# The order of TensorE's work around the last two attention blocks and the first GLU column tiles

## The chip, the cores and the metric

The kernel runs on one core of a Trainium2 chip. The metric is the device time of one execution in microseconds (us); of several executions the median is given. The engines are TensorE (PE, with its weight loads shown apart as PEld), VectorE (DVE), ScalarE (ACT), GpSimd (POOL) and SyncE (SP), which here issues nearly all transfers. Each engine works through its own queue in order and waits for the others by semaphores.

## The reference, cut to what matters

One layer of a decoder for a prompt of 2048 tokens and 32 sample tokens (8 sequences of 4). Attention looks back 128 tokens, so it is done in 16 blocks of 128 tokens, each against its own keys and those of the block before; beside it runs a state-space model (S5) whose output goes through a gated linear unit (GLU). Both are normalised, joined and multiplied by `w_out`; a convolutional FFN follows.

```python
h = _rmsnorm(x, p['norm_mix'])
proj = h @ p['w_in']                       # q, k, v, u
attn, k_win, v_win = attend(q, k, v, sinks)
ssm, h_re, h_im = _s5(u, ...)
ssm = jax.nn.gelu(ssm)
ssm = ssm * jax.nn.sigmoid(ssm @ p['w_glu'] + p['b_glu'])
merged = jnp.concatenate([_rmsnorm(attn, p['g_attn']), _rmsnorm(ssm, p['g_ssm'])], axis=-1)
x = x + merged @ p['w_out']
f, conv_new = _conv_ffn(_rmsnorm(x, p['norm_ffn']), ...)
x = x + f
```

Attention of a block is a softmax with a sink and a distance bias:

```python
s = jnp.einsum('bnqhgd,bnkhd->bnhgqk', qb, kband) * scale
s = s - slopes * dist
s = jnp.where(valid, s, MASK_VALUE)
p = _sink_softmax(s, sinks)
o = jnp.einsum('bnhgqk,bnkhd->bnqhgd', p, vband)
```

## The kernel before

All arrays lie with features on the 128 partitions and tokens along the free axis. A product that must keep more digits than one pass gives is split into a high and a low part of both factors and made in three passes (`mm3`, L89 to L91), so every operand has a "hi" tile, cast by ACT (L83), and a "lo" tile, subtracted by POOL or DVE (L84).

The kernel has stages. First S5's input projection; then a long stage in which q/k/v projections (`qkv`), S5 pairs and attention blocks run mixed; then the GLU, then `wo` (the product with `w_out`), then the FFN's up and down products, which take most of the time. The change lies where the mixed stage runs out into the GLU.

Each kind of work of the mixed stage is a generator, and a table of tokens, `ORDER`, says whose next step is written next: `q` a projection, `s7` a step of S5 pair 7, `a14` a step of attention block 14, `e` a gelu of one channel group, `x` a step of the sample attention, `g` one GLU column tile, `Y`, `T`, `M` and `A` the opening and closing of pools, with the norm of the first merged tile at `M`. PE executes in exactly the order in which the steps are written. The order of the other engines is set by a scheduler from the program's dependencies, so it follows the table, but not word for word.

An attention block (`attention_block`) has five steps. Steps 1 and 2 are the two key/value heads: 12 score matmuls each (`sc_b`) into two PSUM banks of the pool `psa`, which has only these two; DVE adds the bias and takes the maximum (L545); then `softmax` negates the maximum (`ngm`, L510, DVE), takes four exponentials with their sums on ACT (L513, `den`) and one of the sink (L516), adds and inverts on DVE (L517, L518) and multiplies on POOL (L520). `ngm`, `den` and `es` have two buffers each. Steps 3 and 4 transpose the probabilities of a head (`tp_b`, L556, 8 transposes) and copy them out (`pT_b`, L561). Step 5 multiplies by the values (`o`, L567) and ACT copies the result (`osb`, L570, one buffer) for a transfer to `mscr`.

The gelu of a channel group (`gelus`, L947 and L950) reads `y`, writes four buffers `gt`, and sends them to `gscr`. The GLU (`glu_tiles`) runs over 8 token tiles of 260 with 4 column tiles each, 32 steps `g`. For a token tile it loads `gel` (L958, three buffers) from `gscr`, which needs the gelus of all four channel groups, and casts it to `ghi` and `glo`; a column tile is 12 matmuls into one of two PSUM banks, then ACT's tanh (L1029), two DVE operations (L1030, L1031) and a transfer to `mscr` (L1032) from one of three buffers `sg`. The weights of `wo` are loaded in 8 parts (L932); the first three are split by ACT and DVE, the last five by DVE alone (L83, L84). `merged_sums` loads a merged tile (`mt`, L989) and squares it, `merged_norm` makes the factor from a matmul `st_m`, on ACT and DVE.

```python
for tok in ORDER.split():
    ...
    else:
        next(steps[tok])
```

Of the kernel before, what the change touches and what calls it, by code (L numbers as in the profile page):

```python
# [51 lines left out]
a4 s8 a4 a6 s7 a5 s9 q a6 s9 s8 s10 s9 q a5 a5 a6 q a7 s10 s9 s10 q s11 a6 a7 a6 s11 q s11 a7 q s10 s12 a7 a7  # L52
s12 a8 s11 q s13 s12 q q a8 q s13 s12 s13 a8 a9 s14 q a8 s14 a9 q s13 a8 s14 s15 s15 a10 a9 q a9 a9 s15 q s14
a10 q s15 a11 a10 a11 a10 q a10 q q Y a11 a11 a12 a11 q a13 q a12 q a12 q q q e e a12 a13 a12 a14 a13 e e T a13
a13 x g a14 g g x a14 a15 g a14 g g x g a15 x g a14 g g g g a15 g g g g g g g M a15 g g a15 g g g g g g g g g g
g A
"""
WOAT = 9
GELQ = lambda nc: (nc.sync, nc.scalar)[GELQI]
# [1615 lines left out]
```

## Time and profile before

| | us |
|---|---|
| median of 3 runs | 2193.05 (2192.98 to 2195.53) |
| the profiled execution | 2194.39 |
| its span, first to last instruction | 2192.2 |
| PE busy in the span | 2054.4 (94%) |
| DVE, ACT, POOL busy | 1307.6, 1055.8, 1208.9 |

The profile gives a start and a length to every instruction of one execution. A row of a timeline merges like instructions that follow each other; a bracket at its end says how long the engine was idle before and whose work ended that. Names are those of the program without numbers. Matmuls overlap, so the time of one step is best read from the start of one group to the start of the next. A table of stretches gives each engine's busy time, the granted clock of PE (1.00 is 2.4 GHz, 0.50 is 1.2 GHz) and the share of the transfer engines. The chain that ended last is followed back from the last instruction.

### The profile page before, as it was taken

To read this page: it belongs to the slowest core of one execution; us is meant where nothing else is said; L and a number is where in the kernel's file an instruction comes from. 1 tells how busy PE (TensorE), PEld (TensorE's weight loads), DVE (VectorE), ACT (ScalarE), POOL (GpSimd) and SP (SyncE) were. 2 spreads that over 40 slices of the span, in tenths; PEclk is the share of its full clock that TensorE was granted. 3 is DMA by queue.
4 is the path that set the end of the run, shared out by engine and by line. 5 is a ranking of instruction groups with operands and counts; after the bars stand their busy time and mean duration, and the time that the engine had idled before them with its cause. 6 is when DMAs were issued, how large, how long until landed. Compare 5 with 4: busy or idle time off the path is not lost.

```text
span 2192.2 us, 41498 instructions
## 1 busy us (share of the span) xinstructions
PE 2054.4 (94%) x14685; PEld 1923.5 (88%) x14685; DVE 1307.6 (60%) x3298; ACT 1055.8 (48%) x2467; POOL 1208.9 (55%) x1196
## 2 busy tenths in 40 slices
PE   8969999968999979999999998999999999999997
PEld 8967878857998979999999786779999999888997
DVE  8859998458565576766766265227766766601231
ACT  6525465665454456666666332225655655612011
POOL 4857776334356776666665553446666666823121
PEclk9989999989999989999999999999999999999999
DMA  8865434686488733333334795834333333584643
GB/s 232 240 169 158 116 106 138 125 230 189 146 248 258 262 109 109 113 95 109 114 95 128 263 284 170 303 117 157 110 93 108 111 93 108 177 205 125 199 132 95
DMA packets 294352, 347.59 MB, mean 159 GB/s; under 512 B 42344, under 2 KB 250864, under 8 KB 294128
## 3 DMA queue, kind: packets, MB, share of 16 engines
q1 hardware_dynamic: 294144, 344.94, 52.3%
q8 instruction: 116, 1.90, 0.4%
q14 instruction: 92, 0.75, 0.1%
HBM read 232.70 MB, written 107.80 MB: 155 GB/s over the span
## 4 chain that ended last, share of the span: by engine, by line
PE 75%; DVE 8%; DMA 6%; issue 4%; ACT 3%; POOL 3%; SPq 2%; DVEq 0%; ACTq 0%; POOLq 0%
PE ux L1362 21%; PE u L1362 16%; PE dn L90 6%; PE dn L89 6%; PE dn L91 6%; PE wo L90 2%; PE wo L91 2%; PE wo L89 2%; PE qkv L89 2%; PE qkv L91 1%; PE qkv L90 1%; DVE xo L1444 1%; SPq L802 1%; PE u L91 1%; DMA mt<-mscr 1%
## 5 line engine op out<-in xcount | busy, mean ns | idle before, releaser
L84 POOL TENSOR_TENSOR wdl<-wdr,wdh 128x1024 fp32r<-128x1024 f32 x65 | 159.3, 2455 | 287.3 <-ACT wdh L83 272.0
L89 PE MATMUL dn<-ah,wdh 128*128 128x512 f32 (+3 forms) x552 | 205.6, 372 | 8.9 <-DMA ah<-actscr 3.6
L91 PE MATMUL dn<-ah,wdl 128*128 128x512 f32 (+3 forms) x552 | 205.1, 371 | 3.3 <-POOL wdl L84 3.3
L90 PE MATMUL dn<-al,wdh 128*128 128x512 f32 (+3 forms) x552 | 204.9, 371 | 0.5 <-DMA al<-actscr 0.5
L1327 ACT ACTIVATE cc<-u,cw 128x260 f32<-128x260 f32 (+1 forms) x252 | 141.5, 563 | 93.8 <-DVE u L1405 64.1
L1519 DVE TENSOR_TENSOR xo<-xo,dn 128x512 f32<-128x512 f32 (+3 forms) x40 | 21.9, 584 | 265.4 <-PE dn L91 265.1
L83 ACT CAST wdh<-wdr 128x1024 fp32r<-128x1024 f32 x65 | 68.0, 1050 | 230.4 <-PE dn L90 188.4
L84 POOL TENSOR_TENSOR wls<-s,whs 128x1024 fp32r<-128x1024 f32 x42 | 100.9, 2402 | 133.2 <-ACT whs L83 133.2
L1328 DVE SCALAR_TENSOR_TENSOR cc<-u,cw,cc 128x260 f32<-128x260 f32 (+1 forms) x252 | 121.0, 481 | 64.2 <-ACT cc L1327 62.7
L89 PE MATMUL wo<-mh,wo 128*128 128x260 f32 x512 | 149.0, 291 | 2.5 <-ACT mh L83 2.5
L90 PE MATMUL wo<-ml,wo 128*128 128x260 f32 x512 | 146.7, 287 | 1.5 <-POOL ml L84 1.3
L91 PE MATMUL wo<-mh,wo 128*128 128x260 f32 x512 | 146.4, 286 | 0.0
L1405 DVE TENSOR_TENSOR u<-u,cb 128x262 f32<-128x262 f32 x84 | 36.5, 435 | 158.5 <-PE u L1362 158.5
L89 PEld LDWEIGHTS dn<-ah,wdh 128*128 128x128 f32 x552 | 105.1, 190 | 28.7 <-issue 4.0
L91 PEld LDWEIGHTS dn<-ah,wdl 128*128 128x128 f32 x552 | 105.1, 190 | 20.8 <-POOL wdl L84 4.2
L89 PE MATMUL qkv<-hh_p,wqh 128*128 128x256 f32 (+1 forms) x384 | 113.5, 296 | 10.6 <-DVE vs L905 7.4
L84 POOL TENSOR_TENSOR wlt<-s,wht 128x512 fp32r<-128x512 f32 x42 | 54.1, 1288 | 122.6 <-ACT wht L83 64.0
L90 PEld LDWEIGHTS dn<-al,wdh 128*128 128x128 f32 x552 | 105.1, 190 | 17.6 <-DMA al<-actscr 1.0
L1329 DVE SCALAR_TENSOR_TENSOR cc<-u,cw,cc 128x260 f32<-128x260 f32 (+1 forms) x252 | 119.6, 475 | 0.8
L84 POOL TENSOR_TENSOR wlg<-wur,whg 128x1024 fp32r<-128x1024 f32 x42 | 101.1, 2407 | 27.8 <-ACT whg L83 27.8
L520 POOL TENSOR_SCALAR s_b<-s_b,den_b 128x256 f32<-128x256 f32 x128 | 75.4, 605 | 63.2 <-DVE den_b L518 38.4
L90 PE MATMUL qkv<-hl_p,wqh 128*128 128x256 f32 (+1 forms) x384 | 109.9, 286 | 0.0
(574 smaller groups left out, 8370.9 us busy)
## 6 DMA issues: line engine op xcount, KB each, us to landing
actscr<-cc SPq DMA_DIRECT2D x168, 260.0 KB, 4.9
wur<-in_w_up SPq DMA_DIRECT2D x84, 512.0 KB, 4.1
wdr<-in_w_down SPq DMA_DIRECT2D x77, 512.0 KB, 4.9
x<-in_xT SPq DMA_DIRECT2D x56, 256.0 KB, 4.2
hs<-h2scr SPq DMA_DIRECT2D x44, 262.0 KB, 4.6
ah<-actscr SPq DMA_DIRECT2D x42, 256.0 KB, 3.9
al<-actscr SPq DMA_DIRECT2D x42, 256.0 KB, 4.2
mt<-mscr SPq DMA_DIRECT2D x16, 520.0 KB, 5.5
```

The source lines that it names most:

```text
L83: i = nc.scalar.copy(hi, src) if hi_eng is nc.scalar else hi_eng.tensor_copy(hi, src)
L84: return i.ins, lo_eng.tensor_tensor(lo, src, hi.bitcast(F32), ALU.subtract).ins
L89: nc.tensor.matmul(ps, w[0], x[0], start=first, stop=False)
L90: nc.tensor.matmul(ps, w[0], x[1], start=False, stop=False)
L91: nc.tensor.matmul(ps, w[1], x[0], start=False, stop=last)
L520: nc.gpsimd.tensor_scalar(s[:, h], s[:, h], den[:, h : h + 1], 1.0, ALU.mult, ALU.mult)
L802: nc.sync.dma_start(uscr[8 * m + g].rearrange("(s h) c -> h s c", h=16), uperm[m][16 * g : 16 * g + 16])
L1327: nc.scalar.activation(cp, pp[:, 2:], AF.Identity, bias=w[3], scale=w[2])
L1328: nc.vector.scalar_tensor_tensor(cp, pp[:, 1 : npr + 1], w[1], cp, ALU.mult, ALU.add)
L1329: nc.vector.scalar_tensor_tensor(cp, pp[:, 0:npr], w[0], cp, ALU.mult, ALU.add)
L1362: nc.tensor.matmul(pt[:, :W], x[p][:, k], y[q][:, k], start=start and k + i == 0, stop=k == 3 and i == 2, skip_group_check=True)
L1405: v.tensor_tensor(c21[s], c21[s], cb[s][:, 0], ALU.add)
```

## The change

Two lines of `ORDER` are replaced; no other line of the program differs..

```diff
 ...
-a13 x g a14 g g x a14 a15 g a14 g g x g a15 x g a14 g g g g a15 g g g g g g g M a15 g g a15 g g g g g g g g g g
-g A
+a13 a15 a14 a15 a14 a14 g x g a15 a14 g g x g a15 g x g g a15 x g g g g g g g g g g M g g g g g g g g g g g g
+g g A
```

Block 14 has made its first step before these lines and has four left, block 15 all five. Before, the first GLU tile followed block 13's output, and the steps of the two blocks stood one by one between GLU tiles, the last one behind the 21st. Now the three remaining score steps and both transposes of block 14 stand ahead of the first GLU tile, and the last step of either block behind the eighth. The norm of the first merged tile (`M`) stands behind the 18th GLU tile and not behind the 19th; the sample attention's steps move by up to one GLU tile.

On PE, at the place where the mixed stage ends (`o_13` is the output of block 13, `sc_b14_1` the scores of block 14's second head, `tp_` transposes, `glu_0_2` token tile 0, column tile 2, `ssc` the samples' scores; of each group of matmuls its first row), before:

```order
L567 MATMUL o_13_6966<-pT_b13_0_0_6871,vtok_6_0_6141 64x512
L89 MATMUL glu_0_0_7003<-ghi_0_0_6987,wgh0_6926 128x260
L89 MATMUL sc_b14_1_0_7023<-kp10_2167,q0_7_6452 128x256
L89 MATMUL glu_0_1_7057<-ghi_0_0_6987,wgh1_6934 128x260
L89 MATMUL glu_0_2_7075<-ghi_0_0_6987,wgh2_6940 128x260
L604 MATMUL ssc_0_7099<-kc_6978,qs_2188 32x288 x4
L556 MATMUL tp_b14_0_0_7123<-ident_201,s_b14_0_6830 128x128 x4
L89 MATMUL sc_b15_0_0_7139<-kp10_2167,q0_7_6452 128x256
L89 MATMUL glu_0_3_7173<-ghi_0_0_6987,wgh3_6946 128x260
L556 MATMUL tp_b14_1_0_7191<-ident_201,s_b14_1_7021 128x128 x4
L89 MATMUL glu_1_0_7223<-ghi_1_0_7207,wgh0_6926 128x260
```

and now, at the same place:

```order
L567 MATMUL o_13_6966<-pT_b13_0_0_6871,vtok_6_0_6141 64x512
L89 MATMUL sc_b15_0_0_6976<-kp10_2167,q0_7_6452 128x256
L89 MATMUL sc_b14_1_0_7012<-kp10_2167,q0_7_6452 128x256
L89 MATMUL sc_b15_1_0_7048<-kp10_2167,q0_7_6452 128x256
L556 MATMUL tp_b14_0_0_7082<-ident_201,s_b14_0_6830 128x128 x4
L556 MATMUL tp_b14_1_0_7096<-ident_201,s_b14_1_7010 128x128 x4
L89 MATMUL glu_0_0_7126<-ghi_0_0_7110,wgh0_6926 128x260
L89 MATMUL glu_0_1_7157<-ghi_0_0_7110,wgh1_6934 128x260
L556 MATMUL tp_b15_0_0_7175<-ident_201,s_b15_0_6974 128x128 x4
L567 MATMUL o_14_7189<-pT_b14_0_0_7087,vtok_6_1_6145 64x512
L89 MATMUL glu_0_2_7197<-ghi_0_0_7110,wgh2_6940 128x260
L89 MATMUL glu_0_3_7215<-ghi_0_0_7110,wgh3_6946 128x260
```

Three score groups and block 14's transposes have gone from between the GLU tiles to ahead of them.

On ACT, at the same place (the exponentials of blocks 14 and 15, the table load and the gelus of channel group 2), the difference:

```order
 L513 ACTIVATE s_b14_0_6830,den_b14_0_6852<-s_b14_0_6830,ngm_b14_0_6850 128x256 x4
 L516 ACTIVATE es_b14_0_6857<-es_b14_0_6857 128x4
+L513 ACTIVATE s_b15_0_6974,den_b15_0_6996<-s_b15_0_6974,ngm_b15_0_6994 128x256 x4
+L516 ACTIVATE es_b15_0_7001<-es_b15_0_7001 128x4
+L513 ACTIVATE s_b14_1_7010,den_b14_1_7032<-s_b14_1_7010,ngm_b14_1_7030 128x256 x4
+L516 ACTIVATE es_b14_1_7037<-es_b14_1_7037 128x4
+L513 ACTIVATE s_b15_1_7046,den_b15_1_7068<-s_b15_1_7046,ngm_b15_1_7066 128x256 x4
+L516 ACTIVATE es_b15_1_7073<-es_b15_1_7073 128x4
 L947 ACT_TABLE_LOAD
 L947 ACTIVATE gt_2_0_6880<-y_2_6741 128x512
```

Three groups of exponentials now stand ahead of the table load of the gelus, which they followed before.

On DVE, near the end of the GLU (`sg_6_3` is the gate of token tile 6, column 3; `wo06` and `wo16` are the high and low part of the seventh part of `w_out`), before:

```order
L1030 TENSOR_SCALAR sg_6_3_7978<-sg_6_3_7978 128x260
L1030 TENSOR_SCALAR sg_7_0_8012<-sg_7_0_8012 128x260
L1031 TENSOR_TENSOR sg_6_3_7978<-sg_6_3_7978,gel_6_7795 128x260
L1031 TENSOR_TENSOR sg_7_0_8012<-sg_7_0_8012,gel_7_7893 128x260
L83 CAST wo06_8105<-wor6_8107 128x1024
L1030 TENSOR_SCALAR sg_7_1_8030<-sg_7_1_8030 128x260
L84 TENSOR_TENSOR wo16_8106<-wor6_8107,wo06_8105 128x1024
L1031 TENSOR_TENSOR sg_7_1_8030<-sg_7_1_8030,gel_7_7893 128x260
L1117 MEMSET hs_0_0_8884 128x2x2
L83 CAST wo07_8111<-wor7_8113 128x1024
L84 TENSOR_TENSOR wo17_8112<-wor7_8113,wo07_8111 128x1024
L1030 TENSOR_SCALAR sg_7_2_8048<-sg_7_2_8048 128x260
```

and now:

```order
L1030 TENSOR_SCALAR sg_6_1_7942<-sg_6_1_7942 128x260
L1031 TENSOR_TENSOR sg_6_1_7942<-sg_6_1_7942,gel_6_7803 128x260
L83 CAST wo06_8105<-wor6_8107 128x1024
L84 TENSOR_TENSOR wo16_8106<-wor6_8107,wo06_8105 128x1024
L1030 TENSOR_SCALAR sg_6_2_7960<-sg_6_2_7960 128x260
L1030 TENSOR_SCALAR sg_6_3_7978<-sg_6_3_7978 128x260
L1031 TENSOR_TENSOR sg_6_2_7960<-sg_6_2_7960,gel_6_7803 128x260
L1031 TENSOR_TENSOR sg_6_3_7978<-sg_6_3_7978,gel_6_7803 128x260
L83 CAST wo07_8111<-wor7_8113 128x1024
L1117 MEMSET hs_0_0_8884 128x2x2
L84 TENSOR_TENSOR wo17_8112<-wor7_8113,wo07_8111 128x1024
L1030 TENSOR_SCALAR sg_7_0_8012<-sg_7_0_8012 128x260
```

The last two splits of `w_out` have moved from behind the gates of `sg_7_0` and `sg_7_1` to ahead of those of `sg_6_2` and `sg_7_0`.

On SP, at the first column of `wo` (`x2scr` takes the result of that column, `xm` is the residual stream loaded for later columns, `mt_1` the second merged tile), before:

```order
L1193 DMA x2scr_63<-xm_0_0_8138 128x260
L1187 DMA xm_1_4_8715<-in_xT 128x260
L1187 DMA xm_1_5_8744<-in_xT 128x260
L1187 DMA xm_1_6_8799<-in_xT 128x260
L989 DMA mt_1_0_8167<-mscr_62 128x4x260
L989 DMA mt_1_4_8169<-mscr_62 128x4x260
```

and now:

```order
L1032 DMA mscr_62<-sg_7_2_8048 128x260
L1032 DMA mscr_62<-sg_7_3_8066 128x260
L1193 DMA x2scr_63<-xm_0_0_8138 128x260
L989 DMA mt_1_0_8167<-mscr_62 128x4x260
L989 DMA mt_1_4_8169<-mscr_62 128x4x260
```

The three loads of `xm` stand with eight others in one row further up, ahead of the write of `sg_4_2`.

## Rows read from the trace of the kernel before

**Rows 1.** The page: the chain that ended last, shares of the span by engine.

```profile
PE 75%; DVE 8%; DMA 6%; issue 4%; ACT 3%; POOL 3%; SPq 2%; DVEq 0%; ACTq 0%; POOLq 0%
```

**Rows 2.** Timeline of PE: start, length, instruction, count, idle before.

```profile
448.74 3.68 PE L567 MATMUL o<-pT_b,vtok 128*64 128x512 f32 x8
465.57 0.59 PE L89 MATMUL glu<-ghi,wgh 128*128 128x260 f32 x1 [13.14 <-ACT ghi L83]
...
468.69 0.41 PE L89 MATMUL sc_b<-kp,q 128*128 128x256 f32 x1
...
470.62 0.28 PE L89 MATMUL glu<-ghi,wgh 128*128 128x260 f32 x1
...
474.34 1.09 PE L556 MATMUL tp_b<-ident,s_b 128*128 128x128 f32 x8
476.27 0.39 PE L89 MATMUL sc_b<-kp,q 128*128 128x256 f32 x1 [0.83 <-DVE sm L606]
...
477.81 0.28 PE L89 MATMUL glu<-ghi,wgh 128*128 128x260 f32 x1
...
479.25 1.94 PE L556 MATMUL tp_b<-ident,s_b 128*128 128x128 f32 x8
480.94 0.37 PE L89 MATMUL glu<-ghi,wgh 128*128 128x260 f32 x1
```

**Rows 3.** Timeline of ACT, from block 14's exponentials to the second table load.

```profile
444.81 0.51 ACT L513 ACTIVATE s_b<-s_b,ngm_b 128x256 f32<-128x256 f32 x1 [0.32 <-DVE ngm_b L510]
...
446.80 0.19 ACT L516 ACTIVATE es_b<-es_b 128x4 f32<-128x4 f32 x1
447.00 1.28 ACT L947 ACT_TABLE_LOAD   x1
...
455.24 0.58 ACT L570 COPY osb<-o 128x512 f32<-128x512 f32 x1 [2.60 <-DMA mscr<-osb]
456.00 1.12 ACT L947 ACTIVATE gt<-y 128x512 f32<-128x512 f32 x1 [0.18 <-DMA gscr<-gt]
...
457.17 3.11 ACT L947 ACTIVATE gt<-y 128x512 f32<-128x512 f32 x3
...
465.11 1.33 ACT L83 CAST ghi<-gel 128x260 fp32r<-128x260 f32 x4 [4.32 <-DMA gel<-gscr]
...
473.43 1.28 ACT L513 ACT_TABLE_LOAD   x1
```

**Rows 4.** Stretches: length, busy time of each engine (instructions), PE clock, DMA share, GB/s.

```profile
465.57:493.88 28.31, 27.22 (x216) 23.43 (x216) 22.92 (x75) 19.49 (x55) 12.58 (x20) 0.93 0.74 222
493.88:514.17 20.29, 18.14 (x142) 17.11 (x141) 14.37 (x29) 11.68 (x35) 13.28 (x17) 1.00 0.79 231
514.17:547.40 33.23, 26.47 (x179) 22.93 (x177) 30.76 (x53) 16.32 (x37) 13.37 (x16) 0.95 0.55 165
...
466.00:467.00 1.00, 1.00 (x5) 0.97 (x5) 0.00 (x0) 0.44 (x2) 1.00 (x2) 0.50 0.72 196
```

**Rows 5.** Timelines of DVE (first two) and POOL: a reduction, the hole, a normalisation.

```profile
442.26 0.48 DVE L545 CUSTOM_DVE_ANT_0 s_b<-sc_b,bias,sink 128x256 f32<-128x256 f32 x1 [1.59 <-PE sc_b L91]
...
460.82 0.69 DVE L84 TENSOR_TENSOR wgl<-wgraw,wgh 128x512 fp32r<-128x512 f32 x1 [11.20 <-ACT wgh L83]
...
449.81 1.84 POOL L520 TENSOR_SCALAR s_b<-s_b,den_b 128x256 f32<-128x256 f32 x4 [2.38 <-DVE den_b L518]
```

**Rows 6.** DVE's groups from 465.5 to 550: busy us and mean ns, then idle before.

```profile
L561 DVE COPY pT_b<-tp_b 128x512 f32<-128x512 f32 x8 | 5.4, 682 | 0.0
L545 DVE CUSTOM_DVE_ANT_0 s_b<-sc_b,bias,sink 128x256 f32<-128x256 f32 x12 | 5.3, 473 | 0.0
```

**Rows 7.** Timelines of SP (first row) and PE, in the first tile of `wo`.

```profile
551.29 1.61 SPq L1187 DMA_DIRECT2D xm<-in_xT  x3
...
561.11 0.71 PE L115 MATMUL st_m<-ss_m,ones 128*128 128x260 f32 x2 [2.04 <-POOL ss_m L134]
563.55 1.24 PE L115 MATMUL st_m<-ss_m,ones 128*128 128x260 f32 x2 [1.74 <-POOL ss_m L134]
```

## The prediction

> **What bounds the kernel now.** I read the page first: TensorE (PE) holds 75% of the chain that ended last [rows 1], so a change pays only where PE stands still, and only if nothing else is late then. The one large hole in reach of the change is in the timeline of PE: the output matmuls of attention block 13 start at 448.74 and take 3.68 us, and the next thing in PE's order, the first GLU column tile, starts at 465.57 after 13.14 us of idleness put down to ACT's cast of `ghi` [rows 2]. The timeline of ACT tells why [rows 3]: exponentials of block 14 until 446.99, a table load at 447.00, the gelus of channel groups 2 and 3 (with the copy of block 13's output between them, which waits 2.60 us for its buffer to be written back), the last gelu ending at 460.28, and then 4.32 us of waiting until the gelu output has gone to memory and come back as `gel`. So PE waits for a chain of ACT and DMA that begins where the exponentials end. What follows, from 465.57 to the first `wo` matmul at 547.40, has three parts in the table of stretches [rows 4]. Up to 493.88 PE is busy 27.22 of 28.31 us and sets the pace. From there to 514.17 it is busy 18.14 of 20.29. In the last 33.23 us DVE is busy 30.76 and PE only 26.47: DVE sets the pace there, through the GLU gate, the norm of the first merged tile and the splitting of the `wo` weights.
>
> **The change, part by part.** Nothing is added or removed. Three score groups, the transposes of block 14 and, a little, those of block 15 move ahead on PE; the scheduler then places the other engines' work by that order.
>
> *The hole.* PE can start block 15's first scores at 452.42. The hole covers PE's part: twelve score matmuls take 477.81 − 476.27 = 1.54 us at the full clock [rows 2], and DVE is idle there for 11.20 us [rows 5]. It does not cover ACT's part. The order of ACT puts the three groups of exponentials ahead of the gelu table load, and the whole chain to the first GLU tile hangs on that load. First scores of six matmuls are there about 1.1 us after 452.42; four reductions of 0.48 us, a little overlapped [rows 5], end at 455.3; the first reduction of the next group stands ahead of the negated maximum, so the exponentials begin at about 456.2. One group costs ACT 446.99 − 444.81 = 2.18 us [rows 3]; three without a gap would end at 462.8. The third must wait longer, because `den` has two buffers and the first group's is free only after POOL has normalised it: about 459.5 plus 1.84 us [rows 5], so 461.4 + 2.18 = 463.6. The table load thus moves from 447.00 to about 463.6, 16.6 us later. Of this the chain gets back 2.60 + 0.18 us of waiting [rows 3], since block 13's output and the buffers of the gelus are long ready by then: 13.8 us net, and the first GLU tile starts at 479.4. The bounds are 12.2 (no reduction in between, no wait for POOL) and 15.2 (scores at half clock, which cost 470.62 − 468.69 = 1.93 us a group partly at that level [rows 2], and some wait for the gelu buffers remaining). PE still waits some 16 us in place of 13, so its first GLU tile still starts, as before, at a granted clock of 0.50, the lower of the two levels, 1.2 GHz [rows 4].
>
> *The GLU stretch, first part (28.31 us).* It loses a score group of 1.93, the transposes, the wait of 0.83 and the score group from 474.34 to 477.81, 3.47, transposes of 480.94 − 479.25 = 1.69 [rows 2], and a last score group like the one of 1.54: together 8.6 us. It takes in block 15's transposes (two times about 1.0, as the row of 1.09) and output (1.84, half of the 3.68 at half clock), 3.9 us that stood in the later parts. Two waits are new, where the moved scores had been cover: about 1.0 us for the low part of the second weight column, and about 2 us for the sample softmax, whose two ACT operations and table load (1.28 [rows 3]) now follow a cast that needs the third `gel`, itself queued on SP behind block 14's output. So 28.3 − 8.6 + 3.9 + 2.9 = 26.5 us.
>
> *Second part (20.29 us).* It loses one pair of transposes (about 0.8 after overlap) and one GLU tile (1.45), as the norm is now called one column earlier; it gains some wait, since the loads of the first merged tile follow closer on the sample output: bounds 0 and 3, I take 0.5, near zero, because these loads had only small waits before. 18.5 us.
>
> *Third part (33.23 us).* One GLU tile more, transposes and output of block 15 fewer: on DVE that cancels. But in the new order all five weight splits stand ahead of the gate of the last four GLU tiles, where two splits stood behind two of them. One split is about 1.9 us of DVE, so 0 to 3.8 us; I take 1.5, since in the old order, too, one split stood ahead of the last tiles: 34.7 us.
>
> The three parts make 79.7 against 81.83: 2.1 us come back. Behind the first `wo` column SP no longer has three loads of `xm`, 1.61 us, ahead of the loads of the second merged tile, and PE's two waits of 2.04 and 1.74 us for its sums [rows 7] shrink by as much: 1.6 us. The order of all that follows is the same. **Sum: 13.8 − 2.1 − 1.6 = 10.1 us slower.** The span of 2192.2 becomes 2202.3, and the profiled execution's 2194.39 us becomes 2204.5. That execution stands 1.3 us over the median of 2193.05, so I predict 2203.
>
> A rule for such an order: ACT's two table loads at 447.00 and 473.43 cost 1.28 us each [rows 3], and the second serves the exponentials of block 14 and of the samples. The Trainium skill (ScalarE: Activation LUTs, Table sets: the hidden batching unit) asks to batch activation calls by table set, which this change does for block 14 and 15. By that rule a load of 1.28 us would go, and the sum would be 8.8; by the order it stays, as the sample softmax still comes behind the gelus, and I leave the sum at 10.1.
>
> **The rivals.** *Given back.* The stretch returns all 8.6 us of PE work with no new wait, and the delay is at its lower bound: 12.2 − 8.6 − 1.6 = +2.0, to +3.6 with the central delay: 2195 to 2197. For it speaks that DVE loses 5.3 us of reductions and half of the 5.4 us of copies [rows 6]; against it, that most of this work stood in the first part, where PE and not DVE sets the pace.
>
> *Faster.* PE runs the stretch without waits: it is busy 71.8 us in it (the sum of [rows 4]), about 7.8 of that leave, and 81.8 − 64.0 = 17.8 us would come back, with the 1.6 us 19.4: 13.8 − 19.4 = −5.6, some 2187. It decides from the point where the stretch gives back more than 13.8 us. Against it speaks the 30.76 us of DVE in the last part, which the change leaves as they are.
>
> *More is lost.* The bare GLU tiles wait for each other: there are three `sg` buffers, and SP now has eleven loads of `xm`, some 0.54 us each by [rows 7], in one row ahead of the write that frees one of them: up to 5.9 us, so that the stretch gives nothing back or loses some: +14 to +18, 2207 to 2211. The Trainium skill (Perfetto Trace Analysis, Optimization Strategy) says that regimes with different most-contended engines may be run interleaved to advantage; the old order does so with attention and GLU, and by that rule this rival would be the likely one. Rows speak for it only in part: the two regimes are bound by PE and then by DVE [rows 4], but attention lay mostly within PE's.
>
> That the change does not do what it says is excluded: the order of PE shows the three score groups where they are claimed to be.
>
> **How the numbers follow.** The delay seems certain, since the place of the exponentials ahead of the table load is fixed in ACT's order; how much the stretch returns is not. Forecast, +5 to +14 (2198 to 2207): 0.63. Given back: 0.17. More is lost: 0.15. Faster: 0.05. The range of 2195 to 2209 takes in the forecast, most of the second and half of the third. A measurement of this kernel can tell about 0.2%, 4.4 us, from no change: slower by more 0.78, within 0.17, faster 0.05.
>
> **What would show it.** In the profile of the changed kernel: the gelu table load at about 463 in place of 447; the first GLU tile at about 479 after a wait of PE for `ghi` of some 16 us, with nothing of the transposes behind it; the stretch from there to the first `wo` matmul about 80 us; the wait for the sums of the second merged tile under 2.5 us in all; everything behind shifted by the same 10 us. I would be wrong in the first step if the gelus began before 458, in the second if the stretch took under 75 us or over 85.

## The result

The changed kernel takes 2205.8 us (median of six runs, 2202.62 to 2210.42), the kernel before 2194.06 beside it: ratio 1.0052, 95% interval 1.0036 to 1.0067, so 11.7 us slower. Run again in the experiments it was 1.0056 (1.0039 to 1.0074). The forecast was 2203, from 2195 to 2209. The executions of one kernel lie 4 to 21 us apart within a set. The two traces of the changed kernel come from executions of 2208.8 and 2202.8 us, on either side of its median, and differ by 3.4 us in the stretch that matters here; differences of that size between single traces say nothing. Where it matters I use both and several of the old order.

**The hole.** The timeline of PE after, from the second transposes of block 13 to the first GLU tile (columns as in [rows 2]):

```profile
449.12 2.35 PE L556 MATMUL tp_b<-ident,s_b 128*128 128x128 f32 x8 [2.31 <-POOL s_b L520]
...
454.77 0.39 PE L89 MATMUL sc_b<-kp,q 128*128 128x256 f32 x1
...
456.75 0.39 PE L89 MATMUL sc_b<-kp,q 128*128 128x256 f32 x1 [0.28 <-DVE m_b L545]
...
458.78 0.39 PE L89 MATMUL sc_b<-kp,q 128*128 128x256 f32 x1 [0.25 <-DVE m_b L545]
...
464.47 2.69 PE L556 MATMUL tp_b<-ident,s_b 128*128 128x128 f32 x8 [2.95 <-POOL s_b L520]
481.65 0.58 PE L89 MATMUL glu<-ghi,wgh 128*128 128x260 f32 x1 [14.49 <-ACT ghi L83]
```

and of ACT in the same place, where [rows 3] had the load at 447.00:

```profile
458.43 0.51 ACT L513 ACTIVATE s_b<-s_b,ngm_b 128x256 f32<-128x256 f32 x1 [8.45 <-DVE ngm_b L510]
...
463.58 0.51 ACT L513 ACTIVATE s_b<-s_b,ngm_b 128x256 f32<-128x256 f32 x1 [0.81 <-DVE den_b L517]
...
465.77 1.28 ACT L947 ACT_TABLE_LOAD   x1
...
471.27 0.57 ACT L570 COPY osb<-o 128x512 f32<-128x512 f32 x1
471.73 1.12 ACT L947 ACTIVATE gt<-y 128x512 f32<-128x512 f32 x1
...
481.19 2.17 ACT L83 CAST ghi<-gel 128x260 fp32r<-128x260 f32 x6 [4.67 <-DMA gel<-gscr]
```

The three score groups run in the hole, as the change says. ACT then stands idle 8.45 us, does their exponentials and only then loads the gelu table. This execution was already 3.0 us late before the change's place (the transposes of block 13 start at 449.12, before at 446.13), so I measure from there: the first GLU tile comes after 32.53 us in place of 19.44, the hole is 13.1 us longer.

**The rest.** The stretches after, to be held against [rows 4]; the last row reaches from the first `wo` matmul to the first addition of the second token tile:

```profile
481.65:510.76 29.11, 27.34 (x187) 22.04 (x188) 18.95 (x41) 14.96 (x34) 9.31 (x12) 0.83 0.76 225
510.76:532.09 21.33, 17.71 (x122) 17.20 (x121) 10.58 (x23) 11.05 (x27) 9.02 (x12) 0.84 0.79 232
532.09:567.94 35.85, 26.35 (x174) 24.98 (x173) 31.98 (x56) 16.77 (x38) 15.21 (x16) 0.86 0.55 167
567.94:597.07 29.13, 27.24 (x224) 26.77 (x223) 12.52 (x34) 14.33 (x37) 12.58 (x18) 1.00 0.40 125
```

The same in the second trace of the changed kernel:

```profile
478.31:505.44 27.13, 24.43 (x187) 19.09 (x187) 19.66 (x42) 15.04 (x34) 9.31 (x12) 0.94 0.83 250
505.44:523.89 18.45, 15.50 (x122) 14.73 (x121) 11.34 (x21) 10.90 (x27) 9.53 (x12) 1.00 0.84 244
523.89:561.42 37.53, 26.38 (x174) 25.01 (x173) 31.65 (x56) 16.75 (x38) 15.36 (x16) 0.86 0.54 167
561.42:590.31 28.89, 27.26 (x224) 26.79 (x223) 12.50 (x33) 14.86 (x39) 13.01 (x18) 1.00 0.40 126
```

and the last stretch before, which [rows 4] do not have:

```profile
547.40:581.22 33.82, 30.04 (x225) 29.23 (x224) 14.76 (x36) 15.12 (x39) 13.58 (x19) 0.90 0.46 140
```

From the first GLU tile to the second token tile of `wo` that is 115.42 and 112.00 us after, 115.65 before. PE lost work there (8.3 us of busy time in the second trace, 3.2 in the first, where more of it ran at the half clock), but its idle time, length less busy time, rose from 13.8 to 16.8 us, and to 18.4 in the second trace. What PE waits for, before and then after (us in total, times, longest):

```profile
PE glu L89 <- ACT sg L1029: 6.4, 8, 2.2
```

```profile
PE glu L89 <- ACT sg L1029: 12.6, 5, 4.0
```

Eight small waits for the tanh have become five, three of them long, and a stretch behind the first of these shows the half clock (columns as in [rows 4]). In the second trace the same three tiles waited 2.71, 4.80 and 4.85 us.

```profile
523.69 0.58 PE L89 MATMUL glu<-ghi,wgh 128*128 128x260 f32 x1 [3.58 <-ACT sg L1029]
...
540.08 0.58 PE L89 MATMUL glu<-ghi,wgh 128*128 128x260 f32 x1 [4.05 <-ACT sg L1029]
...
558.31 0.58 PE L89 MATMUL glu<-ghi,wgh 128*128 128x260 f32 x1 [3.88 <-ACT sg L1029]
```

```profile
524.00:529.00 5.00, 5.00 (x24) 5.00 (x24) 2.74 (x6) 1.65 (x5) 2.22 (x4) 0.50 0.54 164
530.00:532.00 2.00, 2.00 (x19) 2.00 (x19) 1.60 (x4) 0.56 (x2) 0.52 (x1) 1.00 0.46 141
```

### The profile page after: what moved, and what is told of

It reads as the page before. It is cut to its first block, busy times and chain, and to the rows that moved or that the text cites. A ratio compares the mean times of both kernels' runs of the same rounds, so it can differ in the third digit from the quotient of the medians.

```text
span 2207.0 us, 41497 instructions
## 1 busy us (share of the span) xinstructions
PE 2055.4 (93%) x14685; PEld 1925.7 (87%) x14685; DVE 1308.4 (59%) x3298; ACT 1057.1 (48%) x2467; POOL 1211.0 (55%) x1196
## 4 chain that ended last, share of the span: by engine, by line
PE 60%; DVE 3%; POOL 3%; DMA 2%; issue 2%; ACT 2%; SPq 0%; DVEq 0%; POOLq 0%; ACTq 0%
PE ux L1362 20%; PE u L1362 16%; PE dn L89 7%; PE dn L90 7%; PE dn L91 7%; PE wo L90 1%; PE wo L91 1%; PE wo L89 1%; DVE xo L1444 1%; POOL ml L84 1%; DMA wdr<-in_w_down 1%; DVE xm L1159 0%; POOL wd L84 0%; DMA mt<-mscr 0%; DVE ss_fo L134 0%
## 5 line engine op out<-in xcount | busy, mean ns | idle before, releaser
L91 PE MATMUL qkv<-hh_p,wql 128*128 128x256 f32 (+1 forms) x384 | 110.2, 287 | 0.0
```

The lines of the kernel that those rows point to most:

```text
L91: nc.tensor.matmul(ps, w[1], x[0], start=False, stop=last)
```

## The experiments

My theory after the result had two parts: the exponentials ahead of the gelu table load make the first GLU tile late, and the stretch gives nothing back because bare GLU tiles run into three waits for the tanh. The rivals: a late start itself makes the stretch long; PE sets its pace; VectorE (DVE) does.

One table for all runs. Each ratio is to the kernel before on the same chip. **Hole**: from PE's second transposes of block 13 to its first GLU matmul. **Train**: from there to the end of the last gate (DVE, L1031). **To wo 2**: from the first GLU matmul to DVE's first addition for the second token tile of `wo` (L1192).

| kernel | ratio (95%) | hole | train | to wo 2 |
|---|---|---|---|---|
| before | | 19.44 | 84.57 | 115.65 |
| changed | 1.0052 (1.0036–1.0067) | 32.53 | 87.88 | 115.42 |
| e12 changed again | 1.0056 (1.0039–1.0074) | 32.13 | 84.76 | 112.00 |
| e2 before, gelus delayed | 1.0067 (1.0042–1.0092) | 36.25 | 85.35 | 117.30 |
| e1 changed, gelus first | 1.0037 (1.0024–1.0050) | 22.94 | 92.70 | 121.51 |
| e5 before, one group moved | 1.0054 (1.0042–1.0066) | 25.88 | 90.66 | 120.92 |
| e6 changed, cover at the norm | 1.0049 (1.0032–1.0065) | 33.56 | 85.81 | 113.27 |
| e3 changed, 5 sg | 1.0045 (1.0029–1.0061) | 32.13 | 82.01 | 111.31 |
| e7 changed, squares later | 1.0057 (1.0044–1.0071) | 33.50 | 85.92 | 115.27 |
| e9 e3, e6 and later squares | 1.0061 (1.0043–1.0078) | 32.07 | 86.54 | 117.72 |
| e10 changed, 9.2 us of PE work added | 1.0068 (1.0049–1.0088) | 32.29 | 86.01 | 115.12 |
| e4 before, 5 sg | 0.9999 (0.9987–1.0011) | 17.55 | 86.29 | 115.86 |
| e11 before, PE's idle places filled | 1.0016 (1.0000–1.0032) | 18.34 | 84.70 | 114.15 |
| e13 before, wo splits off DVE | 1.0007 (0.9994–1.0019) | 18.80 | 85.89 | 117.93 |

Hole plus the last column, held against before's 135.09, agrees with the ratios within 3 us (changed: +12.9 beside 11.4), but for e2 and e12, which are 3 to 4 off, and e11 with 6. From the second token tile of `wo` to its last addition all traces take 175 to 178 us: the change is decided by then.

**e2: a delay alone.** The order before; 28 copies on ACT ahead of the gelus of group 2.

```diff
+NDUM = 28
 ...
+                for _ in range(NDUM if (m, i) == (2, 0) else 0):
+                    nc.scalar.copy(gt[:, 0:512].rearrange("p (t c) -> p t c", t=8), y[:, :, 0:64])
```

> The order of the kernel before; 28 added copies of 128x512 on ScalarE ahead of the gelus of channel group 2 delay the chain to the first GLU tile, with nothing moved. At some 0.59 us each they are 16.5 us, less the 2.8 us of waits that the chain had: the first GLU tile 13 to 14 us later. My theory (a delay of the chain goes through to the end in full, and the stretch does not depend on when it begins): stretch 81 to 83 us, time 2206 to 2208, ratio 1.0055 to 1.0065. Rival (a late start makes the stretch itself longer, as in the changed kernel): stretch 86, time 2211 to 2213. Rival (work that does not hang on the chain goes on meanwhile, and part of the delay is given back): 2198 to 2202.

ACT (first two rows) and PE of e2 (its lines behind the edit stand up to three higher):

```profile
453.96 15.55 ACT L949 COPY gt<-y 128x512 f32<-128x512 f32 x24
...
473.10 1.12 ACT L950 ACTIVATE gt<-y 128x512 f32<-128x512 f32 x1 [1.82 <-DMA gscr<-gt]
```

```profile
482.78 0.58 PE L90 MATMUL glu<-ghi,wgh 128*128 128x260 f32 x1 [30.64 <-ACT ghi L84]
```

The copies were dearer than I had reckoned, 0.65 us each and not 0.59, and of the 2.8 us of waits 1.82 remained: the first GLU tile came 16.8 us later. The medians differ by 2211.84 − 2194.96 = 16.9 us. The ratio gives 14.7, because one of the six executions took 2195.82 us, about as long as the kernel before, and the other five 2211.4 to 2215.7; why that one was fast is not known. The time is in the range of the first rival, but not for its reason: the delay was 3 us larger than planned, and the stretch to the first `wo` tile took 83.18 us, near the theory's 81 to 83 and not 86. The train took 85.35 us beside 84.57. So a delay of the gelu chain goes through about in full, and a late start does not make the stretch long by more than two traces differ.

**e1: the gelus first.** The changed order of PE; the three moved softmaxes are held behind the last gelu on ACT.

```diff
+GFIRST = ("b14_1", "b15_0", "b15_1")
 ...
-        softmax(c, pool, s, m, 4, c.sink[:, 4 * kv : 4 * kv + 4], nm)
+        with c.tc.issue_after(c.last_gelu) if nm in GFIRST else nullcontext():
+            softmax(c, pool, s, m, 4, c.sink[:, 4 * kv : 4 * kv + 4], nm)
 ...
```

(The rest of the edit keeps the last gelu as `c.last_gelu`.)

> The order of TensorE is that of the changed kernel; only ScalarE is changed: the exponentials of blocks 15_0, 14_1 and 15_1 are held behind the last gelu. My theory has two parts: the first GLU tile is late because these exponentials stand ahead of the gelu table load, and the stretch from the first GLU tile to the first wo tile is long (86.3 us in the changed kernel, 81.83 before) because the bare GLU tiles run into ScalarE. By it the table load is back at 447 to 450, the first GLU tile starts at 469 to 471 (three groups of 2.18 us and a table load of 1.28 now stand between the last gelu and the casts of gel), the stretch stays at 85 to 87, and the time is some 11 us under the changed kernel's: 2194 to 2197, ratio 1.000 to 1.0015. Rival: the stretch was long because it began late; then it goes back to about 80 and the time is 2187 to 2190. Second rival: something else makes the first GLU tile late, and it stays at about 481, 2205.

ACT (first two rows) and PE of e1 (its lines stand one or two higher):

```profile
449.16 1.28 ACT L949 ACT_TABLE_LOAD   x1
...
470.77 1.94 ACT L84 CAST ghi<-gel 128x260 fp32r<-128x260 f32 x6
```

```profile
468.56 2.69 PE L558 MATMUL tp_b<-ident,s_b 128*128 128x128 f32 x8 [7.72 <-POOL s_b L521]
471.21 0.58 PE L90 MATMUL glu<-ghi,wgh 128*128 128x260 f32 x1
473.99 0.58 PE L91 MATMUL glu<-glo,wgh 128*128 128x260 f32 x1 [2.20 <-DVE glo L85]
...
476.65 0.58 PE L91 MATMUL glu<-glo,wgh 128*128 128x260 f32 x1 [0.99 <-POOL glo L85]
```

The table load is back at 449 and the first GLU tile at 471, as forecast: 9.6 of the 13.1 us came back, so the place of the exponentials made it late. But the gain did not last: 2203.56 us, not 2194 to 2197. The same exponentials now stand ahead of the casts of `gel`, the first tile starts and stops for its low parts, and the train is 92.7 us (90.76 to the first `wo` tile, where 85 to 87 was expected). The hole was one of PE and DVE; ACT's idle times in it, 2.60 us ahead of the last gelus and 4.32 behind them [rows 3], are each too short for three groups of 2.18 us.

**e5: one group.** The order before with only block 15's first scores moved ahead.

```diff
-a13 x g a14 g g x a14 a15 g a14 ...
+a13 a15 x g a14 g g x a14 g a14 ...
```

> The order of the kernel before with one step moved: only the first score group of block 15 goes ahead of the first GLU tile, the other two stay between the tiles. Theory (each group whose exponentials stand ahead of the gelu table load delays the first GLU tile): one group, so the table load at about 458 to 459 in place of 447, the first GLU tile 8 to 10 us later, at 474 to 476; the stretch to the first wo tile loses one score group and stays at 79 to 81; time +6 to +9 over the kernel before: 2201 to 2204, ratio 1.003 to 1.004. Rival (the delay of the changed kernel came from all three groups together, through the wait for POOL and den's two buffers, and one group fits beside the gelus): first GLU tile within 2 us of before, 2193 to 2196.

```profile
473.36 0.58 PE L89 MATMUL glu<-ghi,wgh 128*128 128x260 f32 x1 [19.04 <-ACT ghi L83]
...
487.67 0.33 PE L556 MATMUL tp_b<-ident,s_b 128*128 128x128 f32 x1 [2.33 <-POOL s_b L520]
```

The table load came at 457.84, as forecast, and the hole grew by 6.4 us, less than the 8 to 10 expected and half of what all three groups cost. The time did not follow: 2207.7 us where 2201 to 2204 was expected, ratio 1.0054, as slow as all three groups. The train took 90.66 us; PE waited 2.8 us for block 14's probabilities and 5.0 us for POOL's `glo` in it. So the loss is not one share per group. Why a single group lengthens the train by 6 us is not shown.

**e6, e3, e7, e9: the three waits.** e6 puts block 15's second transposes and output back behind the norm, e3 gives `sg` five buffers, e7 puts the first merged tile's squares later on ACT, e9 does all three (the squares less late, offset −60).

```diff
-... x g a15 g x g g a15 x g g g g g g g g g g M g g g g g g g g g g g g
+... x g g x g g x g g g g g g g g g g M a15 g g a15 g g g g g g g g g g
```

```diff
-                    sg = st.gl2.tile([P, n], F32, tag="sg", name=f"sg_{it}_{m}", bufs=3)
+                    sg = st.gl2.tile([P, n], F32, tag="sg", name=f"sg_{it}_{m}", bufs=5)
```

```diff
+SQP = -400
 ...
-                        st.sums = merged_sums(0, st.ms)
+                        with tc.high_priority(offset=SQP):
+                            st.sums = merged_sums(0, st.ms)
```

> The changed kernel with one piece put back: the second transposes and the output of block 15 stand again behind the norm of the first merged tile (one directly behind it, the other two GLU tiles later), as in the kernel before. My theory: these 3 us of TensorE work covered the time in which ScalarE does the norm's logarithms and exponentials with its two table loads; without them TensorE waited 4.05 us and ran one or two GLU tiles at half clock after it. By it this wait falls under 1 us, the first GLU tile stays at 480 to 482, and the time is 4 to 5 us under the changed kernel's: 2200 to 2202, ratio 1.003. Rival: VectorE sets the pace of the last part (31.98 of 35.85 us busy), and what TensorE does not wait there it waits later: 2204 to 2207, ratio 1.005.

> The changed kernel with five sg buffers in place of three. ScalarE's tanh waited 5.72, 2.48 and about 1 us for the write that frees an sg buffer, and TensorE 3.88 us behind the first of these, with two tiles at half clock after it. Theory A: the ring of three holds TensorE up; the wait of 3.88 goes, and the time is 4 to 6 us under the changed kernel's: 2200 to 2202. Theory B: the tanh is early then, but the gates behind it wait for VectorE, which splits weights: the wait of TensorE goes all the same, since only the tanh frees its bank, but the first merged tile's norm or the wo weights are late instead, and the time moves by less than 2 us: 2204 to 2207.

> The order of TensorE of the changed kernel; the eight squares of the first merged tile stand some four GLU tiles later in the order of ScalarE, where in the changed kernel they stood, waiting for their load, ahead of the tanhs that free TensorE's banks. Theory: the wait of 3.58 us at 523.69 goes, and with it the two GLU tiles at half clock after it; the middle part (to the norm's sums) falls from 21.3 to 16 to 18 us and the first wo tile is 4 to 6 us earlier. In the time a part of this may be given back at the sums of the second merged tile, as with five sg buffers: 2201 to 2204, ratio 1.003 to 1.004. Rival: the sums are then late for the norm, and TensorE waits there as long: 2205 to 2207.

> The changed kernel with all three waits of the stretch treated at once: block 15's second transposes and output back behind the norm, five sg buffers, and the squares of the first merged tile two GLU tiles later on ScalarE. The first GLU tile is as late as in the changed kernel (479 to 482). Theory: the three waits of 3.6 to 4.1 us and the half-clock tiles behind them made the stretch long; it falls from 86.3 to 74 to 77 us, less than the 81.83 of before by the score groups that left it. The sums of the second merged tile then take back some 4 us: time 2198 to 2201, ratio 1.002 to 1.003. Rival: the stretch has a floor of DVE work at about 80 us, and the time is 2203 to 2206.

Each did what it should at its wait: e6 cut the norm's from 4.05 to 1.78 us, e3 the last from 3.88 to 1.74, e7 the first from 3.58 to 0.16. None changed the time by more than the intervals: 2205.3 and 2204.6 us for e6 and e3, as the rival and theory B had said, 2208.4 for e7, above even its rival, and 2211.4 for e9, with all of them (1.0061), above both its ranges. The waits turned up elsewhere: e6 waits 4.30 us at the squares, e3 4.46 and e7 4.84 us at the norm, e9 5.3 us for POOL's `glo`. Only e3's train was clearly shorter in its trace (82.01), and its `wo` part gave much of that back (34.33 us from the first `wo` matmul, 29.13 in the changed kernel). The theory's second part falls: shortening these waits, one by one or together, does not shorten the time.

**e10: PE work added.** The changed kernel with six groups of twelve matmuls that nobody reads, 9.2 us, in pairs ahead of the three tiles that waited.

```diff
-... M g g g g g g g g g g g g
-g g A
+... M
+g g d d g g g g g g g d d g g g g g A
```

(and one pair four tiles ahead of `M`; `d` writes an unread `sc` bank.)

> The changed kernel with six score groups (twelve matmuls of 128x256 each, 1.54 us at the full clock, 9.2 us in all) added on TensorE whose result nobody reads: two ahead of each of the three GLU tiles that waited 3.58, 4.05 and 3.88 us for the tanh. Theory (the stretch is paced by the casts, gates and splits around the GLU tiles; TensorE's work there lies in gaps, so the 6.7 us of score groups and transposes that the change took out brought nothing back): the added 9.2 us cost nothing, and if the half-clock tiles behind the waits count, up to 5 us come back: 2199 to 2206, ratio 1.002 to 1.0055. Rival (TensorE sets the pace): +6 to +9 on the changed kernel, 2212 to 2215, ratio 1.008 to 1.0095.

The last stretch of e10 ahead of `wo` (columns as in [rows 4]), then SP and PE at the start of `wo` (first matmul 561.92):

```profile
532.00:561.92 29.92, 26.13 (x205) 24.86 (x205) 25.08 (x45) 14.39 (x35) 12.91 (x16) 1.00 0.42 130
```

```profile
565.58 0.33 SPq L1032 DMA_DIRECT2D mscr<-sg  x1
...
570.11 1.10 SPq L989 DMA_DIRECT2D mt<-mscr  x2
```

```profile
577.46 1.24 PE L115 MATMUL st_m<-ss_m,ones 128*128 128x260 f32 x2 [3.84 <-POOL ss_m L134]
579.77 1.24 PE L115 MATMUL st_m<-ss_m,ones 128*128 128x260 f32 x2 [1.08 <-POOL ss_m L134]
```

The three waits shrank to 1.24 us at most and the granted clock was 1.00 in the whole last third. PE reached its first `wo` matmul 80.4 us after the first GLU tile, in place of 86.3 and 83.1, with 9.2 us more to do. But the last gate came after 86.0 us all the same, so the last `sg` write and the loads of the second merged tile stood later against PE, and PE waited for their sums. To the second token tile it took 115.12 us. The time, 2210.2 us and 1.0068, lies between the two ranges: above the theory's 2199 to 2206, below the rival's 2212 to 2215. It is 2.6 us by the ratio over the second run of the changed kernel, with intervals that overlap widely; the rival's 6 us more would be 1.0083, which the interval just takes in. So the time alone does not decide; the trace does: 9.2 us more work left the train and the way to the second token tile as long as in the two traces of the changed kernel, within 3.2 us. **PE's work is not what paces the second and third part of the stretch**, so taking it out there could give little back. The first part got no added work.

**e4, e11, e13: other limits, on the kernel before.** e4: five `sg`. e11: ten unread groups, eight in the hole, two at the sums of the second merged tile. e13: five of the ten `wo` split steps of DVE to ACT, two to POOL.

```diff
-a13 x g a14 g g x ...
+a13 d d d d d d d d x g a14 g g x ...
 ...
```

```diff
-WOE = ((1, 1), (1, 1), (1, 1), (1, 1), (1, 1))
+WOE = ((0, 1), (0, 2), (0, 1), (0, 2), (0, 1))
```

> The kernel before with five sg buffers in place of three. Theory: its waits for the tanh in the last part (1.62 and 2.17 us, with a half-clock tile after the second) go, the stretch falls from 81.83 to 77 to 79 us; of this the wait for the sums of the second merged tile takes back half or more, since their loads stand behind the last sg writes in SP's queue: 2191 to 2195, ratio 0.998 to 1.000. Rival: nothing is taken back, 2188 to 2190, ratio 0.997.

> The kernel before with ten unread groups of twelve matmuls added on TensorE only where it stands still: eight in the hole ahead of the first GLU tile (12.3 of its 13.1 us) and one ahead of each of the two sums of the second merged tile (waits of 2.04 and 1.74 us). Theory (the half clock behind these waits is what TensorE pays for its idleness): the first GLU tile takes 1.7 us in place of 3.3, the first wo tile behind the sums 1.6 and 1.6 in place of 3.17 and 2.32: 2 to 4 us off, 2191 to 2193 beside 2195, ratio 0.998 to 0.999. Rival (what follows waits for casts and loads, not for TensorE): no change, 2194 to 2197.

> The order of the kernel before; of the five wo splits in the last part, ScalarE now makes the five high parts and POOL two of the five low parts, which takes some 5.9 us from VectorE (five casts of 0.68, two subtractions of 1.23). In every kernel so far the time from the first GLU tile to the end of the last gate was 82 to 93 us and in most of them 84 to 88, whatever TensorE had to do in between. Theory (VectorE paces the last part, 30.76 of 33.23 us busy before): that time falls from 84.6 to 79 to 82 us, and as the loads of the second merged tile stand behind the last sg write, their sums and the time follow: 2189 to 2192, ratio 0.9975 to 0.999. Rival (the train of GLU tiles is paced by the chain tanh, gate, write and cast as a whole, not by VectorE's load): 84 to 86 us still, 2193 to 2196; if POOL's low parts delay its own glo and sums, up to 2198.

The last stretch before `wo` in e13:

```profile
514.72:549.00 34.28, 27.14 (x179) 23.06 (x177) 28.14 (x45) 20.07 (x42) 18.43 (x18) 0.95 0.52 159
```

DVE is busy 28.14 us there in place of 30.76 [rows 4], ACT and POOL are busy 3.8 and 5.1 us more, and the train is 85.89 beside 84.57. So nothing shows that VectorE's load paces it, but the test is a weak one: of the 5.9 us that were to go, 2.3 went from the time up to the first `wo` tile, in part because the gates' first operation (L1030) took DVE 16.1 us in all and not 13.8. e4 and e13 are no different from before, e11 not faster: its `wo` stretch ran at a clock of 1.00 and was 1.7 us shorter, and the median did not show it. No version beat the kernel before.

> The changed kernel again, beside the others on one chip, for a second trace of it. By the medians and traces so far: first GLU tile 32 to 33 us after the transposes of block 13 (19.4 before), from there to the second row of wo tiles about as long as before (115.4 against 115.65 us), 2205 to 2208, ratio 1.004 to 1.0065.

e12 is the changed kernel itself; its rows stand above. The hole, 32.13 us, and the time, 2206.8 us, came as expected; the way to the second token tile was 112.00 us and not 115.4.

## Why the prediction was right, point by point

**Step 1, the hole: right.** Forecast +13.8 us (12.2 to 15.2); measured 32.53 and 32.13 against 19.44, so 13.1 and 12.7 (and up to 15.0 against the holes of e4, e11 and e13, which are 17.55 to 18.80). The inner terms held too: the table load 15.8 us later (18.8 less the 3.0 of a late start) where I had 16.6; the third group's wait 0.81 us, to 463.58 (the row names DVE's L517; POOL's normalisation of the first group, which frees the `den` buffer, ends at 463.55); the waits of 2.60 and 0.18 us [rows 3] gone; nothing of the transposes left behind the wait for `ghi`, which was 14.49 and 14.24 us where I had some 16. e2 shows that such a delay reaches the end in full, e1 that the exponentials' place is its cause.

**Step 2, the stretch: the sum too good, its ground not borne out.** I let 2.1 us come back, from 81.83 to 79.7; it took 86.29 and 83.11. By my own bound of 85 the first trace says that this step was wrong, the second does not. By parts: 26.5, 18.5 and 34.7 forecast, 29.11, 21.33 and 35.85 in the first trace, 27.13, 18.45 and 37.53 in the second, where only the third part is off. What the sum had at nothing there is PE's two waits for the tanh behind the norm: 4.05 and 3.88 us in one trace, 4.80 and 4.85 in the other, while before the longest in that part were 1.62 and 2.17.

The ground was that "PE and not DVE sets the pace" in the first part, from which I took PE's work off the time there, and DVE in the last. In the first part PE's busy time went from 27.22 to 24.43 us in the second trace, and the part became only 1.2 us shorter. In the other two e10 shows that PE's work is not the pace, and e13 gives no sign that DVE's load is. From the first GLU tile to the last gate the 32 tiles take 84.6 to 87.9 us in eleven of fourteen traces, with PE work removed, added, at full or half clock; the others are e3 with 82.01, e5 with 90.66 and e1 with 92.70. I take that for the pace of the chain of cast, matmul, tanh, gate and write as a whole. This is argued and not shown, and which link holds it the runs do not settle.

**Step 3, the first `wo` tile: right in kind, too small.** Forecast 1.6 us; from 33.82 to 29.13 and 28.89 it was 4.7 and 4.9. The loads of the second merged tile do come 1.66 us earlier against the first `wo` matmul, 3.96 in place of 5.62 us (SP, rows below), and the waits of 2.04 and 1.74 us [rows 7] became 0 and 1.89. What I left out is the clock, 0.90 in that stretch before and 1.00 in both traces after: behind two waits the two halves of the next `wo` tile took 3.17 and 2.32 us, behind one 1.79 and 1.61.

```profile
571.47 0.32 SPq L1193 DMA_DIRECT2D x2scr<-xm  x1
571.90 0.97 SPq L989 DMA_DIRECT2D mt<-mscr  x2
```

```profile
581.94 0.70 PE L115 MATMUL st_m<-ss_m,ones 128*128 128x260 f32 x2 [1.89 <-POOL ss_m L134]
```

Steps 2 and 3 are not apart: whatever brings PE to `wo` sooner (e3, e10) finds the loads held by the last gate and pays there. Together I had 3.7 us returned; the two traces show 0.2 and 3.65, and the medians (11.7 and 13.2 us slower, with a hole 13 us longer) rather little. So the sum came out right because its one large term was right. That it came out so close is luck in part: step 2 was 6.6 and 3.4 us too good in the two traces, step 3 3.1 and 3.3 us too small, so in the second trace the two errors cancel and in the first half of the larger one is left.

**The rivals.** *Faster* needed 17.8 us back and *given back* 8.6 with no new wait; neither came: PE's waits for the tanh doubled. *More is lost* named the wait for an `sg` buffer. ACT did wait 9.3 and 11.5 us in all for `sg` writes in the two traces, with one of 5.72 and one of 6.70, but before it had waited 9.4, in smaller pieces; the eleven loads of `xm`, at 533.96 to 539.19, are over, in the first trace, long before the first of these waits, which ends at 557.77; and e3 widened the ring to five without a clear change of time. The Trainium skill (Perfetto Trace Analysis, Optimization Strategy) says that a gap which repeats can mean too few buffers for the next tile; here the gaps repeat, and more buffers shortened one of them and not the time. Its rule in the same section, that regimes may gain from being interleaved, fits the traces: in the old order attention stood between the GLU tiles of a train of 84.57 us, and without most of it the train takes 87.88 and 84.76. No run tests the rule apart from the hole.

**ScalarE's tables.** The table load that a batching by sets might have saved stayed: both orders have one gelu load and one for the exponentials, at 473.43 before [rows 3] and, for the sample softmax, at 496.77 after.

## What to carry to other kernels

A hole in one engine is room only for work whose other halves fit too. Before filling PE's hole, follow what each filled-in matmul releases: here its exponentials entered ACT's queue ahead of the very chain that PE was waiting for. And before counting on removed work to come back, ask whether the stretch is shorter at all when that engine has less to do; adding unread work there is a direct test.

## What the runs showed of the hardware

The half clock was dearer in rows than in time. Three of PE's idle places in e11 were filled and the granted clock rose from 0.90 to 1.00 in the `wo` stretch, and in e10 from 0.86 to 1.00 in the last part of the GLU, yet neither kernel was measurably faster. The first GLU tile of e11 ran at 1.00 and PE's next step still began only 3.09 us after it, as at 0.50 before, 3.12 us [rows 2]. A wait's length alone did not tell what follows: in the changed kernel's two traces the same tile started after 3.58 us of waiting at a clock of 0.50, and after 2.71 us at 1.00, while before a wait of 2.17 us ahead of a GLU tile was followed by 2.97 us for that tile, the half clock. The second trace behind the wait of 2.71 us (columns as in [rows 4]):

```profile
517.60:520.60 3.00, 3.00 (x25) 3.00 (x26) 2.90 (x6) 1.57 (x5) 1.79 (x3) 1.00 0.85 254
```
